# Two closing norms ordered anew, and returned rows gathered into the ring: a two-layer diffusion trunk with routed experts on one core

## The chip, the cores and the metric

The kernel runs on one core of a Trainium2 chip. It is one launch that computes the whole model below. The metric is the device time of a run in microseconds (us). A core has five engines that run their own instruction streams and wait for each other by semaphores: TensorE (PE in the profile: matrix products and transposes, results in PSUM), VectorE (DVE), ScalarE (ACT), GpSimd (POOL) and SyncE (SP, which here only issues transfers). Transfers (DMA) are issued from a queue of an engine (SPq, ACTq, POOLq) and run beside the engines.

## The reference, cut to what matters

There are 512 latent tokens and 256 context tokens of 1024 features, 32-bit floats, two layers. Layer 0 mixes tokens by windowed attention, layer 1 by a gated MLP over chunks of 128 tokens (gMLP); each is followed by a mixture of 16 experts in which each token goes to two.

```python
for i in range(DEPTH):                      # DEPTH = 2
    ...                                     # the mixer, its residual and norm
    y = routed_moe(tokens, router_w, router_bias, moe_w1[i], moe_w3[i], moe_w2[i])
    x = layer_norm(ALPHA * x + g_f * y[-B * L:].reshape(B, L, D), ln2_g[i], ln2_b[i])

def routed_moe(...):
    ...
    def expert_block(args):
        xb, e = args
        return (jax.nn.silu(xb @ w1[e]) * (xb @ w3[e])) @ w2[e]
    ys = lax.map(expert_block, (xs, blk_expert)).reshape(P, D)
    return jax.ops.segment_sum(ys * row_gate[:, None], row_tok, num_segments=T + 1)[:T]

def layer_norm(x, g, b):
    mu = mean(x); var = mean(square(x - mu))
    return (x - mu) * rsqrt(var + 1e-5) * g + b

def chunk_gmlp(h, w_in, b_in, ...):         # layer 1's mixer, h = x * (1 + scale) + shift
    z = gelu(h @ w_in + b_in)
    u, v = z[..., :1024], z[..., 1024:]
    ...
```

What matters here is the second norm of each layer ("closing norm"): it takes the sum of a token's residual and the two rows that its experts gave, and writes the normalised token. After layer 0 the gMLP's projection of `v` comes next; after layer 1 the result is the output.

## The kernel before, in words

**Tiles.** The 512 latent tokens are four tiles `X[0]` to `X[3]` of 128 tokens x 1024 features, held in SBUF (`x` in the rows). SBUF buffers come from pools: `slot` gives one of 28 buffers of 128 x 1024 ("the ring", for weights, split halves and much else), `uslot` one of 8 others. PSUM has three kinds of buffers, `pa` (128 x 1024), `pb` and `pt` (128 x 512), two of each.

**Experts.** `moe` (L1113 on) goes over a fixed list of units, each a number of rows for one expert: `gemm1`, `glu`, `gemm2` (`py`, a `pb` or `pa` buffer). The results of all units but the last two are multiplied by the gate (`ys`) and stored from POOL to a DRAM table `ydr` (L1070 to L1075). At unit n-2 `collect` (L1097) issues eight indirect DMAs on POOL: for each of the two experts of a token (`a` = 1, then `a` = 0) and each tile, the rows of the table that belong to its tokens come into a buffer `y`. They can start when the last store has landed. `combine` (L1106) is a DVE instruction per tile and `a`: X += y x gate; `a` = 1 stands before the last unit's `gemm2` in the program, `a` = 0 after it.

**The last two units** are not stored. Their result, times the gate (`ys`, L1154 for unit n-2 and L716 for n-1), is brought to the tokens by products with a one-hot matrix `oT` (`rows`, L681 to L685), two per tile for each of the two units, accumulated in PSUM; in the program and in PE's order those of unit n-2 (u = 0) come right behind that unit's work, those of unit n-1 (u = 1) behind `ys` of L716.

**The closing norm** (`last_norm`, L670). Per tile: two DVE additions of the PSUM halves to X with a running sum (`add`, L692), the mean (`mean`, L696), two squares with a sum on ACT (L699), the variance on DVE (`var`, L704 and L705). Then a reciprocal square root by Newton steps on DVE (`newton`, L730 to L742, some 14 tiny instructions), done for two tiles at a time (`norm`), and the normalisation on ACT: L1360 in layer 0, L1422 in layer 1.

**Behind the norm of layer 0** stands `pre(t)` for each tile: eight PE transposes (L1327) in two halves, a scale and shift out of PSUM on DVE (L1335, `ht`), a cast to the rounded type on ACT (L1339, `gh`), the remainder on DVE (L1340, `gl`), and two POOL instructions that apply the norm's own gain and bias to X (L1341, L1342). `vhalf(t, n)` is the projection of tile t to one half of `v`: 24 products (L428 to L430) over the eight blocks of features, three for each: `gh` x `wh`, `gh` x `wl`, `gl` x `wh`. The weights `winv` come in eight pieces; `split` (L221) casts a piece on ACT (`wh`, L224) and subtracts on DVE (`wl`, L225). Pieces 0 to 3 serve n = 0.

**Behind the norm of layer 1** the gain is multiplied on DVE (L1423) and the bias added (L1424): tiles 0 and 1 on POOL, tiles 2 and 3 on DVE. Then the output is stored from SP.

**What sets the order.** A scheduler of the tile framework orders each engine's stream by its own cost estimates; where `in_order` encloses code (all of `last_norm`, and `pre` and `vhalf` of n = 0), the named engines keep the program's order. SP issues weight pieces in a fixed list, as far as `limit` and the free buffers allow.

## Time and profile before

| | |
|---|---|
| median of 3 runs | 1209.11 us (1207.64 to 1211.41) |
| profiled execution | 1208.63 us, span from first to last instruction 1206.9 us |
| mean granted TensorE clock | 0.922 of full speed (2.4 GHz) |
| busy share of the span | PE 86%, PEld 49%, DVE 50%, ACT 29%, POOL 21% |
| DMA | 330.42 MB, mean 274 GB/s |
| closing norm of layer 0 | about 676 to 707 us, PE idle from 689.9 to 704.3 |
| closing norm of layer 1 | about 1166 us to the end, PE idle from 1173.6 |

The busy share is a mean over stages. The two closing norms are the two stretches late in a layer in which PE, elsewhere almost always busy, has nothing to do, so what ends there is read from the timeline of each engine and not from the shares. In a timeline row the first two numbers are the start and the busy time in us, counted from the span's start; `xN` is the number of instructions that the row joins; the bracket is the idle time before it and what ended it.

### The profile page before, as it was taken

Reading aid. Unit: us, or ns where it says so; the run is one execution under the profiler, and the core shown is the slowest. Engines: PE = TensorE matmul, PEld = TensorE weight load, DVE = VectorE, ACT = ScalarE, POOL = GpSimd, SP = SyncE. Lnnn points to the kernel's source line nnn. Section 1 sums busy time; section 2 is a strip of 40 time slices with the busy share of each in tenths; the row PEclk is TensorE's granted clock in tenths of the full one; section 3 lists DMA queues with packets and bytes.
Section 4 is the critical chain, followed back from the end, with each engine's and each line's share of the span. In section 5 each row is a group of like instructions: output and inputs, shape, how many; then the busy total and the mean of one; then the engine's idle time right before and its main releaser. Section 6 shows DMA issues by size and latency. Waiting matters only on the chain. (4 is left out here: it accounts for less than half of the span.)

```text
span 1206.9 us, 17614 instructions
## 1 busy us (share of the span) xinstructions
PE 1043.0 (86%) x6216; PEld 596.6 (49%) x6216; DVE 607.2 (50%) x1540; ACT 353.2 (29%) x716; POOL 253.0 (21%) x241
## 2 busy tenths in 40 slices
PE   6789778898898697999999769999859899999980
PEld 2567655554576233444344247888723344433430
DVE  1798899768346731211212597655565121221137
ACT  1553366776433111111101153532211011111103
POOL 0044424425000112331110343000011222211131
PEclk9898869999899798999999869999969899999995
DMA  8945776474467797999999803236489994899981
GB/s 337 402 152 179 263 271 189 139 259 166 137 217 283 253 384 259 390 410 410 410 410 410 293 1 140 88 101 208 177 307 412 347 410 160 351 410 409 410 329 70
DMA packets 103525, 330.42 MB, mean 274 GB/s; under 512 B 13040, under 2 KB 23744, under 8 KB 103424
## 3 DMA queue, kind: packets, MB, share of 16 engines
q1 hardware_dynamic: 88336, 287.43, 62.6%
q0 software_dynamic: 10512, 27.28, 6.1%
q10 hardware_dynamic: 4576, 14.45, 3.3%
q8 instruction: 53, 0.87, 0.3%
q14 instruction: 48, 0.39, 0.1%
HBM read 310.19 MB, written 22.06 MB: 275 GB/s over the span
## 5 line engine op out<-in xcount | busy, mean ns | idle before, releaser
L1031 PE MATMUL pb<-ring,xt 128*32 128x256 f32 (+1 forms) x1824 | 225.6, 467 | 11.5 <-DVEq L1253 10.8
L1031 PEld LDWEIGHTS pb<-ring,xt 128*32 128x32 f32 (+1 forms) x1824 | 83.3, 121 | 130.6 <-issue 83.9
L1042 DVE TENSOR_TENSOR si<-si,pb 128x256 f32<-128x256 f32 (+1 forms) x43 | 15.7, 365 | 223.2 <-ACT si L1041 223.2
L1075 POOL DMA_DIRECT2D ydr<-ys x114 | 58.1, 516 | 315.1 <-DVE ys L1070 229.9
L1064 PE MATMUL pb<-ring,hh 128*32 128x256 f32 (+1 forms) x912 | 113.2, 462 | 0.5 <-ACT hh L1053 0.5
L360 POOL TENSOR_TENSOR raw<-raw,row 128x1024 f32<-128x1024 f32 x28 | 78.2, 2801 | 108.7 <-DMA raw<-in_mt 81.1
L358 DVE SCALAR_TENSOR_TENSOR raw<-raw,row 128x1024 f32<-128x1024 f32 x52 | 91.0, 1764 | 0.0
L1041 ACT ACTIVATE si<-pb 128x256 f32<-128x256 f32 (+1 forms) x43 | 14.6, 339 | 232.5 <-PE pb L1031 232.5
L1031 PE MATMUL pa<-ring,xt 128*128 128x512 f32 x160 | 72.4, 600 | 0.0
L1064 PEld LDWEIGHTS pb<-ring,hh 128*32 128x32 f32 (+1 forms) x912 | 39.6, 119 | 58.3 <-issue 43.4
L994 POOL DMA_INDIRECT xg<-hdr,Rgi x22 | 23.2, 1056 | 213.6 <-DVE peb L868 124.6
L225 DVE TENSOR_TENSOR wl<-raw,wh 128x1024 fp32r<-128x1024 f32 x44 | 56.7, 1318 | 9.2 <-ACT wh L224 9.1
L558 DVE TENSOR_SCALAR_CACHE_REDUCE P<-pa,nsink 128x512 f32<-128x512 f32 (+1 forms) x64 | 50.9, 811 | 20.2 <-PE pa L554 8.1
L1053 ACT COPY hh<-pt 128x256 f32<-128x256 f32 (+2 forms) x48 | 17.0, 354 | 147.5 <-PE pt L1051 147.5
L1013 DVE TENSOR_SCALAR xt<-pt,gc,bc 128x128 f32<-128x128 f32 x88 | 30.1, 404 | 51.5 <-PE pt L1005 51.5
L560 ACT ACTIVATE P<-P,nm 128x512 f32<-128x512 f32 (+1 forms) x64 | 49.5, 775 | 14.3 <-DVE P L558 14.1
L1070 DVE TENSOR_TENSOR ys<-pb,gfs 128x512 f32<-128x512 f32 (+1 forms) x39 | 22.1, 567 | 58.4 <-PE pb L1064 58.4
L1011 ACT ACTIVATE xt<-pt,bc,gc 128x128 f32<-128x128 f32 x88 | 33.1, 456 | 59.5 <-PE pt L1005 38.9
L1031 PEld LDWEIGHTS pa<-ring,xt 128*128 128x128 f32 x160 | 29.1, 190 | 40.1 <-issue 39.9
L593 PE MATMUL pt<-cc,P 128*128 128x128 f32 x288 | 45.4, 290 | 4.0 <-ACT PT L594 3.6
L593 PEld LDWEIGHTS pt<-cc,P 128*128 128x128 f32 x288 | 32.4, 146 | 31.6 <-issue 26.0
L594 ACT COPY PT<-pt 128x512 f32<-128x512 f32 x72 | 39.4, 580 | 28.7 <-PE pt L593 28.7
(366 smaller groups left out, 2046.1 us busy)
## 6 DMA issues: line engine op xcount, KB each, us to landing
ring<-in_moe SPq DMA_DIRECT2D x336, 512.0 KB, 10.6
raw<-in_mt SPq DMA_DIRECT2D x80, 512.0 KB, 5.3
raw<-in_moe SPq DMA_DIRECT2D x48, 512.0 KB, 6.5
raw<-in_mod SPq DMA_DIRECT2D x16, 512.0 KB, 10.2
raw<-in_qkv SPq DMA_DIRECT2D x12, 512.0 KB, 10.2
ydr<-ys POOLq DMA_DIRECT2D x42, 128.0 KB, 5.4
ydr<-zero SPq DMA_DIRECT2D x10, 512.0 KB, 8.0
raw<-in_wo SPq DMA_DIRECT2D x8, 512.0 KB, 5.3
```

The lines of the kernel that those rows point to most:

```text
L225: V.tensor_sub(lo, src, hi.bitcast(F32))
L358: V.scalar_tensor_tensor(w, w, 1.0, srow[0], op0=OP.mult, op1=OP.mult, accum_out=mv[l][:, j:j + 1])
L360: GP.tensor_mul(w, w, srow[0])
L558: V.tensor_scalar(P[j], reg, -0.125, nsink[:, p * 8 + j:p * 8 + j + 1], op0=OP.mult, op1=OP.min, accum_out=nm[:, j:j + 1])
L560: SC.activation(P[j], P[j], AF.Exp, bias=nm[:, j:j + 1], scale=-1.0, accum_out=sums[:, j:j + 1])
L593: PE.transpose(pt[:, j * 128:(j + 1) * 128], P[a * 4 + j][:, i * 128:(i + 1) * 128], idf)
L594: cp = SC.copy(tl[:, a, :], pt)
L1011: SC.activation(o, i, AF.Identity, bias=b, scale=g)
L1013: V.tensor_scalar(o, i, g, b, op0=OP.mult, op1=OP.add)
L1031: PE.matmul(o.rearrange("p (m c) -> p m c", m=2), xt[:, k, c:c + n], w[:, h], start=(k == 0), stop=(k == 7), skip_group_check=True)
L1064: PE.matmul(o, ht[f], w[:, h], start=(f == 0), stop=(f == 3), skip_group_check=True)
L1075: GP.dma_start(ydr[row:row + n, h * n * 8:(h + 1) * n * 8], ys[h * n:h * n + n, :])
```

## The change

There are four parts.

1. **Layer 0, weights.** Pieces 0 to 3 of `winv` are loaded and split ahead of the gathers in the program. The SP loads of pieces 4 to 7 wait until the last gather (`got`) has landed.
2. **Buffers.** In layer 1 the gathered rows of `a` = 1 go to the ring (`slot`), not to `uslot`.
3. **Order inside the closing norm.** `combine` and both `ys` are moved into `last_norm`, in one fixed DVE order: four combines (`a` = 1), `ys` of unit n-2, two combines (`a` = 0), `ys` of unit n-1, two combines. The one-hot products of unit n-2 come behind its `ys`, so behind the first four combines.
4. **What follows the sums** is a function of the layer. `middle` (layer 0): sums of tiles 0 to 2, the norm of tiles 0 and 1, sums of tile 3, the norm of tiles 2 and 3. `end` (layer 1): sums of all tiles, one Newton chain for four tiles; z = (X - mean) x gain before the chain's result is known, then z x rstd + bias, both DVE; tile 1's last step is done on PE as bias (through the identity) plus a diagonal matrix of rstd times z, and copied out by ACT. The POOL additions and ACT normalisations of layer 1 are gone.

```diff
@@ issue (SP's weight list)
             wdma[0] = SP.dma_start(t, src)
+            if p[0] == "winv" and p[1] > 3:
+                after(wdma[0], RT[0]["got"], mybir.DependencyClass.Sync)
@@ moe
-        limit[0] = len(pieces) if l else pos["winu", 0]
+        limit[0] = len(pieces) if l else pos["winv", 4]
...
             elif i == n - 2:
-                R["yp"] = slot([128, 512], F32, "ys")
-                V.scalar_tensor_tensor(R["yp"], py, R["gs"][:, 0:1], gf[64], op0=OP.mult, op1=OP.mult)
+                R["py"] = py
...
             if i == n - 2:
-                collect(l, 1, uslot)
+                for p in [("winv", j) for j in range(4) if not l]:
+                    issue(pos[p] + 1)
+                    pairs[p] = split(raws[p])
+                collect(l, 1, slot if l else uslot)
                 collect(l, 0, slot)
-            if i == n - 1:
-                combine(l, 1, X)
+                limit[0] = max(limit[0], pos["winu", 0])
...
-        combine(l, 0, X)
@@ last_norm
         with in_order(PE, V, SC):
-            V.scalar_tensor_tensor(ys, py, R["gs"][:, 1:2], gf, op0=OP.mult, op1=OP.mult)
-            for t in range(4):
-                rows(t, 1, ys)
-            for t in range(4):
-                add(t, 0)
-                add(t, 1)
-                mean(t)
-            r = norm(0), norm(1)
-        return r
+            combine(l, 1, X, 0, 4)
+            for u, p in enumerate((R["py"], py)):
+                V.scalar_tensor_tensor(ys[u], p, R["gs"][:, u:u + 1], gf, op0=OP.mult, op1=OP.mult)
+                for t in range(4):
+                    rows(t, u, ys[u])
+                if u == 0:
+                    combine(l, 0, X, 0, 2)
+            combine(l, 0, X, 2, 4)
+            finish(X, sums, norm, nmu)
@@ layer 0
+    def middle(X, sums, norm, nmu):
+        def pair(t):
+            y = norm(t, t + 2)
+            nmr = small([128, 2], F32, "xm")
+            V.tensor_mul(nmr, nmu[:, t:t + 2], y)
+            for i in range(2):
+                SC.activation(X[t + i], X[t + i], AF.Identity, bias=nmr[:, i:i + 1], scale=y[:, i:i + 1])
+        for t in range(3):
+            sums(t)
+        pair(0)
+        sums(3)
+        pair(2)
@@ layer 1
-            SC.activation(x, x, AF.Identity, bias=nmr[:, i:i + 1], scale=y[:, i:i + 1])
-            V.tensor_mul(x, x, g2)
-            (GP if t == 0 else V).tensor_add(x, x, b2)
-            SP.dma_start(out[0, (t + i) * 128:(t + i + 1) * 128, :], x)
+    def end(X, sums, norm, nmu):
...
+        def scaled(t):
+            V.scalar_tensor_tensor(z[t], X[t], nmu[:, t:t + 1], g2, op0=OP.add, op1=OP.mult)
+        def done(t, y):
+            V.scalar_tensor_tensor(z[t], z[t], y[:, t:t + 1], b2, op0=OP.mult, op1=OP.add)
+            SP.dma_start(out[0, t * 128:(t + 1) * 128, :], z[t])
+        for t in range(4):
+            sums(t)
+        p = psA()
+        for ns in halves:
+            PE.matmul(p[:, ns], idf, b2[:, ns], start=True, stop=False, skip_group_check=True)
+        scaled(0)
+        scaled(1)
+        y = norm(0, 4)
+        V.tensor_scalar(dg, idf, y[:, 1:2], None, op0=OP.mult)
+        for ns in halves:
+            PE.matmul(p[:, ns], dg, z[1][:, ns], start=False, stop=True, skip_group_check=True)
+        done(0, y)
+        for ns in halves:
+            SC.copy(o[:, ns], p[:, ns])
+        SP.dma_start(out[0, 128:256, :], o)
+        for t in (2, 3):
+            scaled(t)
+            done(t, y)
```

How the instructions stand now, at three places. First DVE in the closing norm of layer 0, before (x_2832 to x_2835 are the four token tiles, L225 the subtraction of a weight piece, L1110 a combine, L1154 and L716 the two `ys`):

```order
L1154 SCALAR_TENSOR_TENSOR ys_6525<-pb_6516,gs_6253,gfs_3404 128x512
L225 TENSOR_TENSOR wl_6556<-raw_6420,wh_6555 128x1024
L225 TENSOR_TENSOR wl_6560<-raw_6424,wh_6559 128x1024
L1110 SCALAR_TENSOR_TENSOR x_2832<-y_6459,pg_5494,x_2832 128x1024
L225 TENSOR_TENSOR wl_6564<-raw_6428,wh_6563 128x1024
L225 TENSOR_TENSOR wl_6568<-raw_6432,wh_6567 128x1024
L716 SCALAR_TENSOR_TENSOR ys_6599<-pb_6536,gs_6253,gfs_3404 128x512
L1110 SCALAR_TENSOR_TENSOR x_2833<-y_6463,pg_5494,x_2833 128x1024
L1110 SCALAR_TENSOR_TENSOR x_2834<-y_6467,pg_5494,x_2834 128x1024
L1110 SCALAR_TENSOR_TENSOR x_2835<-y_6471,pg_5494,x_2835 128x1024
L1110 SCALAR_TENSOR_TENSOR x_2832<-y_6475,pg_5494,x_2832 128x1024
L1110 SCALAR_TENSOR_TENSOR x_2833<-y_6479,pg_5494,x_2833 128x1024
```

and after the change (the same are L227, L1112 and L720):

```order
L227 TENSOR_TENSOR wl_6452<-raw_6420,wh_6451 128x1024
L227 TENSOR_TENSOR wl_6456<-raw_6424,wh_6455 128x1024
L227 TENSOR_TENSOR wl_6460<-raw_6428,wh_6459 128x1024
L227 TENSOR_TENSOR wl_6464<-raw_6432,wh_6463 128x1024
L1112 SCALAR_TENSOR_TENSOR x_2832<-y_6467,pg_5494,x_2832 128x1024
L1112 SCALAR_TENSOR_TENSOR x_2833<-y_6471,pg_5494,x_2833 128x1024
L1112 SCALAR_TENSOR_TENSOR x_2834<-y_6475,pg_5494,x_2834 128x1024
L1112 SCALAR_TENSOR_TENSOR x_2835<-y_6479,pg_5494,x_2835 128x1024
L720 SCALAR_TENSOR_TENSOR ys_6588<-pb_6532,gs_6253,gfs_3404 128x512
L1112 SCALAR_TENSOR_TENSOR x_2832<-y_6483,pg_5494,x_2832 128x1024
L1112 SCALAR_TENSOR_TENSOR x_2833<-y_6487,pg_5494,x_2833 128x1024
L720 SCALAR_TENSOR_TENSOR ys_6589<-pb_6546,gs_6253,gfs_3404 128x512
```

The four subtractions stand together ahead of the combines; the `ys` of unit n-2 has moved from the front to behind four combines. The same order of combines and `ys` holds in layer 1, without the weights.

Second, PE in the projections that follow, before (L1327 is the transpose; pb_6753 is tile 0's half, pb_6810 tile 1's):

```order
L429 MATMUL pb_6753<-wl_6568,gh_6582 128x512
L430 MATMUL pb_6753<-wh_6567,gl_6583 128x512
L1327 MATMUL pt_6780<-cc,x_2834 128x128 x4
L428 MATMUL pb_6810<-wh_6555,gh_6576 128x512
L429 MATMUL pb_6810<-wl_6556,gh_6576 128x512
L430 MATMUL pb_6810<-wh_6555,gl_6577 128x512
L428 MATMUL pb_6810<-wh_6555,gh_6576 128x512
```

and after (L1329 the transpose; pb_6809 is tile 1's half, pb_6866 tile 2's):

```order
L431 MATMUL pb_6809<-wl_6464,gh_6572 128x512
L432 MATMUL pb_6809<-wh_6463,gl_6573 128x512
L1329 MATMUL pt_6779<-cc,x_2834 128x128 x4
L1329 MATMUL pt_6793<-cc,x_2834 128x128 x4
L430 MATMUL pb_6866<-wh_6451,gh_6566 128x512
L431 MATMUL pb_6866<-wl_6452,gh_6566 128x512
L1329 MATMUL pt_6836<-cc,x_2835 128x128 x4
```

Before, tile 2's first transposes stand ahead of tile 1's products and its second ones fourteen rows further, among them. Now both stand behind the last product of tile 1, and the next products are those of tile 2 itself. ACT's normalisation of tiles 2 and 3 has moved as well, behind the first gelu.

Third, DVE at the end of layer 1, before (L741, L742 and L712 end the second Newton chain; L1423 is the gain, L1424 the bias):

```order
L741 SCALAR_TENSOR_TENSOR xny_11278<-xnu_11283,xny_11278 128x2
L742 TENSOR_SCALAR xny_11278<-xny_11278 128x2
L712 TENSOR_TENSOR xm_11294<-xn_11196,xny_11278 128x2
L1423 TENSOR_TENSOR x_2834<-x_2834,row_11191 128x1024
L1423 TENSOR_TENSOR x_2835<-x_2835,row_11191 128x1024
L1424 TENSOR_TENSOR x_2834<-x_2834,row_11193 128x1024
L1424 TENSOR_TENSOR x_2835<-x_2835,row_11193 128x1024
```

and after (L743 and L744 end the only chain, width 4; L1454 is the diagonal, L1438 `scaled`, L1441 `done`):

```order
L743 SCALAR_TENSOR_TENSOR xny_11269<-xnu_11274,xny_11269 128x4
L744 TENSOR_SCALAR xny_11269<-xny_11269 128x4
L1454 TENSOR_SCALAR dg_11227<-cc,xny_11269 128x128
L1441 SCALAR_TENSOR_TENSOR z_11222<-z_11222,xny_11269,row_11182 128x1024
L1438 SCALAR_TENSOR_TENSOR z_11224<-x_2834,xn_11185,row_11180 128x1024
L1441 SCALAR_TENSOR_TENSOR z_11224<-z_11224,xny_11269,row_11182 128x1024
L1438 SCALAR_TENSOR_TENSOR z_11225<-x_2835,xn_11185,row_11180 128x1024
L1441 SCALAR_TENSOR_TENSOR z_11225<-z_11225,xny_11269,row_11182 128x1024
```

Two full-width instructions per tile are left on DVE for tiles 2 and 3 behind the chain, one for tile 0 and none for tile 1.

## Rows read from the trace of the kernel before

**Rows 1.** The chain of waits at the end: start us, length us, what

```profile
1191.14 2.23 DVE xny L741
...
1193.39 2.27 DVE xnu L739
```

**Rows 2.** Timeline of POOL at the end of layer 1

```profile
1190.02 5.61 POOL L1424 TENSOR_TENSOR x<-x,row 128x1024 f32<-128x1024 f32 x2 [18.55 <-DVE xnu L740]
```

**Rows 3.** Timeline of DVE at the end of layer 1

```profile
1166.58 0.75 DVE L716 SCALAR_TENSOR_TENSOR ys<-pb,gs,gfs 128x512 f32<-128x512 f32 x1 [2.68 <-PE pb L1064]
...
1169.32 8.96 DVE L1110 SCALAR_TENSOR_TENSOR x<-y,pg,x 128x1024 f32<-128x1024 f32 x7 [0.28 <-DMA y<-ydr,prow]
...
1178.20 0.69 DVE L692 SCALAR_TENSOR_TENSOR x<-pa,x 128x512 f32<-128x512 f32 x1
...
1184.07 0.20 DVE L704 TENSOR_SCALAR xv<-xq 128x1 f32<-128x1 f32 x1
...
1184.80 0.17 DVE L730 TENSOR_SCALAR xny<-xv 128x2 int32<-128x2 int32 x1
...
1187.18 0.16 DVE L712 TENSOR_TENSOR xm<-xn,xny 128x2 f32<-128x2 f32 x1
...
1200.68 2.35 DVE L1424 TENSOR_TENSOR x<-x,row 128x1024 f32<-128x1024 f32 x2
```

**Rows 4.** Timeline of PE, L684: warm in layer 1, cold in layer 0

```profile
1166.46 1.99 PE L684 MATMUL pa<-ys,oT 64*128 64x512 f32 x8
...
682.43 1.22 PE L684 MATMUL pb<-ys,oT 64*128 64x512 f32 x1 [2.89 <-DVE ys L716]
...
688.47 1.45 PE L684 MATMUL pb<-ys,oT 64*128 64x512 f32 x3
```

**Rows 5.** Windows: length, engines' busy time, granted clock, DMA share, GB/s

```profile
682.00:683.00 1.00, 0.57 (x2) 0.51 (x4) 1.00 (x2) 0.00 (x0) 0.58 (x1) 0.50 1.01 414
...
1176.00:1178.00 2.00, 0.00 (x0) 0.00 (x0) 2.00 (x2) 0.00 (x0) 0.00 (x0) 0.62 0.04 16
```

**Rows 6.** Timeline of SPq, POOL and ACT ahead of layer 0's norm

```profile
648.45 10.52 SPq L208 DMA_DIRECT2D raw<-in_winv  x8
...
662.55 0.54 POOL L1072 DMA_DIRECT2D ydr<-ys  x1 [13.55 <-DVE ys L1070]
...
671.26 1.06 POOL L1102 DMA_INDIRECT y<-ydr,prow  x1 [8.17 <-DMA ydr<-ys]
...
672.99 1.04 ACT L224 CAST wh<-raw 128x1024 fp32r<-128x1024 f32 x1 [1.11 <-issue]
```

**Rows 7.** The page, section 6: issues, KB each, median us to landing

```profile
ydr<-ys POOLq DMA_DIRECT2D x42, 128.0 KB, 5.4
```

**Rows 8.** Timeline of DVE in layer 0's norm

```profile
674.07 2.42 DVE L225 TENSOR_TENSOR wl<-raw,wh 128x1024 fp32r<-128x1024 f32 x2 [0.79 <-ACT wh L224]
...
678.16 1.28 DVE L1110 SCALAR_TENSOR_TENSOR x<-y,pg,x 128x1024 f32<-128x1024 f32 x1 [1.66 <-DMA y<-ydr,prow]
...
692.72 0.68 DVE L692 SCALAR_TENSOR_TENSOR x<-pa,x 128x512 f32<-128x512 f32 x1
...
699.66 0.20 DVE L704 TENSOR_SCALAR xv<-xq 128x1 f32<-128x1 f32 x1
```

**Rows 9.** Timeline of PE, DVE and POOL behind layer 0's norm

```profile
704.32 1.97 PE L1327 MATMUL pt<-cc,x 128*128 128x128 f32 x8 [14.41 <-ACT x L1360]
...
711.74 1.35 DVE L1335 TENSOR_SCALAR ht<-pt,gc,bc 128x128 f32<-128x128 f32 x4
...
716.14 3.38 DVE L1340 TENSOR_TENSOR gl<-ht,gh 128x256 fp32r<-128x256 f32 x2 [0.87 <-ACT gh L1339]
...
716.32 0.60 PE L1327 MATMUL pt<-cc,x 128*128 128x128 f32 x4
...
716.79 2.45 POOL L1342 TENSOR_TENSOR x<-x,row 128x1024 f32<-128x1024 f32 x1
...
719.58 0.50 PE L430 MATMUL pb<-wh,gl 128*128 128x512 f32 x1 [0.81 <-DVE gl L1340]
```

More of the change, by code (lines that the diff above doesn't have):

```diff
@@ L235, in ensure_split @@
                     return
-            else:
+            elif p not in pairs:
                 issue(nsplit[0] + 1)
@@ L668, in in_order, with last_norm @@
                     before[e] = i
-    def last_norm(l, X, py, gf):
+    def last_norm(l, X, py, gf, finish):
         R = RT[l]
@@ L675, in last_norm @@
         q = small([128, 4, 2], F32, "xq", 1)
-        v = [small([128, 3, 2], F32, "xv") for _ in range(2)]
+        v = small([128, 3, 4], F32, "xv", 1)
         o = [psA(), psA(), psT(), psT()]
         o = [[o[0][:, :512], o[0][:, 512:]], [o[1][:, :512], o[1][:, 512:]], o[2:], [psB(), psB()]]
-        ys = slot([128, 512], F32, "ys")
+        ys = [slot([128, 512], F32, "ys") for _ in range(2)]
         def rows(t, u, y):
@@ L685, in rows @@
                           start=(u == 0), stop=(u == 1))
-        for t in range(4):
-            rows(t, 0, R["yp"])
         def add(t, n):
@@ L702, in var, with norm, sums @@
         def var(t):
-            w = v[t // 2][:, 0, t % 2:t % 2 + 1]
+            w = v[:, 0, t:t + 1]
             V.tensor_scalar(w, q[:, t, 0:1], q[:, t, 1:2], 1.0 / D, op0=OP.add, op1=OP.mult)
             V.tensor_scalar(w, w, EPS, None, op0=OP.add)
-        def norm(i):
-            var(2 * i)
-            var(2 * i + 1)
-            y = newton([v[i][:, k] for k in range(3)], "x", 2)
-            nmr = small([128, 2], F32, "xm")
-            V.tensor_mul(nmr, nmu[:, 2 * i:2 * i + 2], y)
-            return y, nmr
-        with in_order(PE, V, SC):
-            V.scalar_tensor_tensor(ys, py, R["gs"][:, 1:2], gf, op0=OP.mult, op1=OP.mult)
-            for t in range(4):
-                rows(t, 1, ys)
-            for t in range(4):
-                add(t, 0)
-                add(t, 1)
-                mean(t)
-            r = norm(0), norm(1)
-        return r
+        def norm(a, b):
+            for t in range(a, b):
+                var(t)
+            return newton([v[:, k, a:b] for k in range(3)], "x", b - a)
+        def sums(t):
+            add(t, 0)
+            add(t, 1)
+            mean(t)
+        with in_order(PE, V, SC):
+            combine(l, 1, X, 0, 4)
[7 more added lines that the diff above has]
+            finish(X, sums, norm, nmu)
     def newton(v, w, n=1):
-        y = small([128, n], F32, w + "ny")
+        y = small([128, max(n, 4 * (n > 1))], F32, w + "ny")[:, :n]
         yi = y.bitcast(I32)
@@ L733, in newton @@
         V.tensor_scalar(v[2], v[0], 0.0625, None, op0=OP.mult)
-        u = small([128, n], F32, w + "nu")
+        u = small([128, max(n, 4 * (n > 1))], F32, w + "nu")[:, :n]
         for i in range(3):
@@ L1101, in collect, with combine @@
             R["y", t, a] = alloc([128, D], F32, "y")
-            GP.indirect_dma_start(out=R["y", t, a], out_offset=None, in_=ydr[:ZR[l] + 1, :],
-                                  in_offset=bass.IndirectOffsetOnAxis(ap=R["row"][:, a, t:t + 1], axis=0),
-                                  bounds_check=ZR[l], oob_is_err=False)
-    def combine(l, a, X):
+            R["got"] = GP.indirect_dma_start(out=R["y", t, a], out_offset=None, in_=ydr[:ZR[l] + 1, :],
+                                             in_offset=bass.IndirectOffsetOnAxis(ap=R["row"][:, a, t:t + 1], axis=0),
+                                             bounds_check=ZR[l], oob_is_err=False)
+    def combine(l, a, X, t0, t1):
         R = RT[l]
-        for t in range(4):
+        for t in range(t0, t1):
             V.scalar_tensor_tensor(X[t], R["y", t, a], R["g"][:, a, t:t + 1], X[t], op0=OP.mult, op1=OP.add)
@@ L1356, in vnorm @@
         SC.activation(v, v, AF.Identity, bias=nmr, scale=rstd)
-    for t, (y, nmr) in zip((0, 2), last_norm(0, X, py, gf)):
-        for i in range(2):
-            SC.activation(X[t + i], X[t + i], AF.Identity, bias=nmr[:, i:i + 1], scale=y[:, i:i + 1])
+    def middle(X, sums, norm, nmu):
[10 more added lines that the diff above has]
+        pair(2)
+    last_norm(0, X, py, gf, middle)
     with in_order(V, SC):
```

8 lines of the change are left out of this document (5 added, 3 removed).

## The prediction, made before the changed kernel was run

> **What bounds the kernel now.** I read the chain of waits first, then the timeline of each engine over the two closing norms, then windows for the clock and the transfers.
>
> The end of layer 1 is a DVE chain. In the chain of waits two instructions of two elements per partition hold 2.23 and 2.27 us [rows 1], where their like, the instruction that ends a Newton chain, takes 0.16 [rows 3]. In the same stretch POOL runs its two additions, 5.61 us from 1190.02 [rows 2], and the two DVE instructions end with POOL's. So DVE is held by POOL's work. The whole stretch from the first sum at 1178.20 to the last addition at 1200.68 + 2.35 = 1203.03 is 24.83 us [rows 3]; what follows (the last store) is 1206.9 - 1203.03 = 3.9 and stays.
>
> PE has no work in these stretches, and its clock shows it. At 682 to 683 it is granted 0.50, the lower of the two levels (1.2 GHz), after a wait of 2.89 us; at 1176 to 1178, with PE out of work, the mean is 0.62 [rows 4, 5]. At the full level four pairs of one-hot products take 1.99 us. At the lower one the stretch from 682.43 to 688.47 + 1.45 = 689.92 holds nine pairs in 7.49 us, the last of them fast again: some 0.84 a pair [rows 4].
>
> Layer 0's norm begins with transfers. The last store to the table is issued at 662.55, and the first gather begins 8.7 us later, released by its landing [rows 6], where the median store takes 5.4 [rows 7]: eight weight pieces were issued on SP from 648.45 on [rows 6]. The first combine still waits 1.66 us for its rows, and the sums start at 692.72 [rows 8]. PE, with nothing to do for 14.41 us, starts the transposes at 704.32 when ACT has normalised [rows 9]; from there PE is the bound, almost without gaps.
>
> **The change in layer 1: what it removes.** Counted behind the first sum. Four tiles of sums are unchanged: 1184.07 - 1178.20 = 5.87 us. Two `scaled` now stand next; seven combines, an instruction of the same shape and two SBUF inputs, take 8.96, so 1.28 each and some 1.2 without a wait: 2.4. They hide ACT's squares of the last tile. The variance costs 0.73 for two tiles (1184.07 to 1184.80), so 1.4 for four. One chain: 1187.18 - 1184.80 = 2.38; a width of four instead of two is not priced higher, since 0.16 for 128x2 is all overhead (bounds 0 and 0.5). The diagonal: 0.3. Then five full instructions, 6.1. Sum 5.9 + 2.4 + 1.4 + 2.4 + 0.3 + 6.1 = 18.5, so 6.3 us less than 24.83 [rows 3]. Of this 4.2 is the lock by POOL (2.23 + 2.27 - 2 x 0.16), the rest the second chain and the shorter tail. Tile 1's products and copies lie beside the five DVE instructions; without that cover they would cost some 3 us.
>
> **What it adds there.** The order of DVE is now four combines, `ys`, two combines, `ys`, two combines. Before, unit n-2's products ran right behind PE's last projection at 1166.46, at full clock [rows 4], beside the combines. Now they wait for `ys` behind the fourth combine: the second starts at 1169.32, so the fourth ends about 1173.2 and `ys` (0.75) at 1173.9 [rows 3]. PE has then been idle for over 7 us, longer than the 2.89 after which it was granted 0.50 [rows 4, 5]. So I take the low level: eight pairs at 0.84 make 6.7, the first tile's pairs of unit n-1 another 0.8, and the first sum starts at about 1181.5 instead of 1178.20: +3.3. Behind the waiting products stand only the next ones, and DVE's sums wait for them. The bounds: with PE not in the way DVE alone adds one `ys` twice, +1.5; with every pair slow to the last tile +5. Layer 1 together: -6.3 + 3.3 = -3.0 (from -4.8 to -1.3).
>
> **Layer 0, the front.** Weight pieces 4 to 7 are 2.1 MB, at the 414 GB/s of the window [rows 5] 5.1 us of transfers, and they leave the way of the store and the gathers. The store can win at most 8.7 - 5.4 = 3.3; I take 2.5 (bounds 0 and 3.3). The casts start about 1 us earlier, since the row loads that kept ACT before 672.99 [rows 6] now stand behind them, and the four subtractions, 2.42 a pair [rows 8], are done by 677.8. Then 4.9 for four combines and 0.75 for `ys`: 683.5. PE is cold as it was at 682.43: 6.7 for the block, 0.8 for tile 0: sums from 691.2. Before, they started at 692.72, with one more combine (1.2) still to come between, so 693.9 is what compares: -2.7. The norm of the first pair after three tiles instead of four saves one tile of sums, 5.87 / 4 = 1.5. The transposes start 4.2 earlier. SP's new wait has only pieces 4 to 7 behind it; they are used some 30 us later, and cost nothing.
>
> **Layer 0, the middle.** Tile 3's sums now delay ACT's normalisation of tile 2, and the scheduler has answered: both transposes of tile 2 stand behind the last product of tile 1, and tile 2's own products right behind them. Before, the first of them ran at 716.32 under tile 1's products, and the chain from a transpose to a product was hidden: the scale, 1.35 for four, a cast, a subtraction [rows 9]. Now PE waits for it, some 1.3 beyond what tile 3's transposes fill. And a subtraction was held when POOL's bias ran: a pair took 3.38 beside POOL's 2.45, some 2.4 more than free, and PE lost only 0.81 of it since it had other products [rows 9]. POOL's two instructions for tile 2 start as soon as its last transpose is done, now exactly when PE waits for these subtractions. I count one lock: 1.3 + 2.4 = 3.7. Bounds: 0 (all of it beside other work) and 6.1 (two locks). Layer 0 together: -4.2 + 3.7 = -0.5. Its bounds: with the store quickest (3.3 instead of 2.5) and no loss in the middle -5.0; with no gain by the store, so only the order's 1.5, and the middle as taken +2.2.
>
> The page SBUF — State Buffer of the Trainium skill, section Who interferes with whom, says that a DVE instruction with two SBUF inputs contends with a GpSimd instruction that reads SBUF, and that the one that comes second is fully blocked. The held DVE instructions of [rows 1, 9] agree. It speaks for the end of layer 1, where POOL's additions go, and against the middle of layer 0; by it alone each of tile 2's POOL instructions could hold a subtraction.
>
> **Sum.** -3.0 - 0.5 = -3.5 us against the profiled execution's 1208.63 (1206.9 span and 1.7 around it). The median of the runs is 0.5 above that execution, so 1209.11 - 3.5 = 1205.6. The rest of the trace keeps its order and is costed at nothing; ring buffers for layer 1's gathers are free at that point, since all weights have been loaded.
>
> **Rivals.**
> - *PE's one-hot products are not in the way* (the clock holds or they overlap better). For: at the full level eight pairs fit in 3.5 us, less than the four combines and two `ys` behind which they stand. Against: 0.50 after a shorter idle [rows 4, 5]. Layer 1 then wins 4.8, layer 0 another 1.7 more, 2.2: together -7.0, 1202.1.
> - *Layer 0's gathers come no sooner.* For: the store may wait for its own queue and not for the weights, and eight gathers are 4.2 MB by themselves. Against: 8.7 beside 5.4. Then the front wins only the 1.5 of the order, and layer 0 is +2.2, in all -0.8: 1208.3.
> - *Slower: POOL holds the subtractions of tiles 2 and 3 again and again.* Four POOL instructions meet eight subtractions there; three locks more than the one I count cost 3 x 2.4 = 7.2, and -3.5 + 7.2 = +3.7: 1212.8. From the second one on the change has lost its gain. For: a pair of 3.38 with PE waiting behind it [rows 9]. Against: between two POOL instructions DVE gets in, and only the first product of a block waits at once.
> - That the change does not do what it says is excluded by the order of the instructions for all but the wait for the last gather, which is the second rival.
>
> **How the numbers follow.** The forecast 0.42, PE not in the way 0.20, gathers no sooner 0.18, locks 0.17, something else 0.03. A measurement can tell about 0.3%, 3.6 us: faster is below 1205.5, slower above 1212.7. Of the forecast's own range, 1202.9 to 1208.3, half is faster. Faster: 0.21 + 0.20 = 0.41. Same: 0.21 + 0.18 + half of the locks 0.06 = 0.45. Slower: the other locks 0.11 and 0.03 = 0.14. The range from 1200.5 to 1211.0 leaves out the locks' upper part and the last of the first rival.
>
> **What would show it.** Right: no POOL addition and no tiny DVE instruction above 0.3 us behind layer 1's sums; 18 to 19 us from the first sum to the last DVE instruction; a granted clock of 0.50 in unit n-2's products of both layers, and a first sum there at 1181 on the old time base. In layer 0 a first gather some 2.5 us sooner behind the store, transposes about 4 sooner, and then a gap of PE of some 3 us behind tile 2's transposes. It is wrong if PE runs those products at the full level, if the middle shows no gap or several, or if layer 1's tail does not shrink by 6.

## The result, and the profile after

The changed kernel takes 1214.19 us (median of 7 runs, 1211.9 to 1214.97) against 1207.64 for the kernel before (7 runs); the ratio is 1.0056, with a 95% interval of 1.0035 to 1.0077. It is slower, by some 6.5 us. 1205.6 had been predicted, with a range up to 1211.0 and 0.14 for slower.

The profiled execution has a span of 1210.0 us, 3.1 more than before. The first 674 us were 1.9 shorter in this execution; the difference is there from 473 us on, long before the first transfer that the change moves (646 us). So I compare two stretches that begin with the end of PE's last expert product in a layer (`gemm2`; 675.91 and 674.05 in layer 0, 1166.54 and 1171.90 in layer 1), in us:

| stretch | before | after | predicted |
|---|---|---|---|
| layer 0: to the first transpose | 28.4 | 29.6 | 24.2 |
| layer 0: from there to the first product of the second half of `v` ("the middle") | 31.7 | 38.8 | 35.4 |
| layer 1: to the first sum | 11.7 | 14.9 | 15.0 |
| layer 1: first sum to last DVE instruction | 24.8 | 18.6 | 18.5 |
| layer 1: from there to the end | 3.9 | 4.6 | 3.9 |
| sum of the five | 100.5 | 106.5 | 97.0 |

Layer 1 came out as worked out, layer 0 did not.

**The end of layer 1.** DVE's timeline after the change, the rows that answer to [rows 3] (start, busy time, then as there):

```profile
1178.63 0.74 DVE L720 SCALAR_TENSOR_TENSOR ys<-pb,gs,gfs 128x512 f32<-128x512 f32 x1
...
1186.78 0.69 DVE L692 SCALAR_TENSOR_TENSOR x<-pa,x 128x512 f32<-128x512 f32 x1 [1.97 <-PE pa L687]
...
1198.88 0.29 DVE L1454 TENSOR_SCALAR dg<-cc,xny 128x128 f32<-128x128 f32 x1
...
1204.11 1.28 DVE L1441 SCALAR_TENSOR_TENSOR z<-z,xny,row 128x1024 f32<-128x1024 f32 x1
```

From 1186.78 to 1204.11 + 1.28 there is no tiny instruction of over 0.3 us left; [rows 1, 2] have no counterpart. The first sum waits 1.97 us for PE (its row above). PE's products of unit n-2 start only behind the fourth combine, after 7.53 us of idle time, at the lower clock level:

```profile
1179.43 3.79 PE L687 MATMUL pa<-ys,oT 64*128 64x512 f32 x8 [7.53 <-DVE ys L720]
...
1185.71 1.88 PE L687 MATMUL pa<-ys,oT 64*128 64x512 f32 x8
```

The window over them, with the columns of [rows 5], shows a granted clock of 0.50:

```profile
1180.00:1182.00 2.00, 2.00 (x6) 0.68 (x4) 2.00 (x3) 0.00 (x0) 0.00 (x0) 0.50 0.58 231
```

The sixteen records of unit n-2 take 6.28 us (1179.43 to 1185.71), where [rows 4] show eight of them in 1.99 at the full level. The prediction put 3.3 on this step; it measured 3.2. Of these, 1.97 is the wait for PE; the other 1.2 is DVE's own, whose last combine ends 12.9 us behind PE's last expert product instead of 11.7.

**Layer 0's front.** DVE, PE and ACT up to the first square:

```profile
675.55 2.47 DVE L1112 SCALAR_TENSOR_TENSOR x<-y,pg,x 128x1024 f32<-128x1024 f32 x2
678.87 1.28 DVE L1112 SCALAR_TENSOR_TENSOR x<-y,pg,x 128x1024 f32<-128x1024 f32 x1 [0.84 <-DMA y<-ydr,prow]
682.30 1.28 DVE L1112 SCALAR_TENSOR_TENSOR x<-y,pg,x 128x1024 f32<-128x1024 f32 x1 [2.15 <-DMA y<-ydr,prow]
...
684.30 3.79 PE L687 MATMUL pa<-ys,oT 64*128 64x512 f32 x8 [10.24 <-DVE ys L720]
...
687.98 8.28 ACTq L1122 DMA_DIRECT2D gfs<-mdr  x6
...
693.09 0.21 DVE L696 TENSOR_SCALAR xn<-xs 128x1 f32<-128x1 f32 x1
...
696.30 0.72 ACT L699 ACTIVATE sq<-x,xn 128x512 f32<-128x512 f32 x1 [22.50 <-DVE xn L696]
```

Two things were not foreseen. The third and fourth combine wait 0.84 and 2.15 us for gathered rows, and PE's products stand behind the fourth, so the first sum comes 0.3 us sooner than the like of [rows 8] and not 2.7 (17.7 behind PE's last expert product, against 16.8 with a combine of 1.2 still to come). And the first square starts 3.0 us behind the first mean, which is there at 693.09 + 0.21: ACT stands in six issues of transfers from 687.98 to 696.26. They load the next layer's gate row (`gfs`, L1122), whose buffer the last `ys` reads.

**Layer 0's middle.** PE's waits there, in a view that sums them (us in total, times, longest), before and after (9.4 of the first line after are the wait ahead of the first transpose, so outside the middle):

```profile
PE pb L430 <- DVE gl L1340: 1.3, 2, 0.8
```

```profile
PE pt L1329 <- ACT x L1366: 9.9, 2, 9.4
PE pb L432 <- DVE gl L1342: 3.9, 6, 0.9
PE pb L430 <- ACT gh L1341: 0.8, 1, 0.8
...
PE pt L1329 <- DVE ht L1337: 0.7, 1, 0.7
```

These waits explain only a part of the 7.1 us. PE's idle time in the middle rose from 1.7 to 6.4 us, its busy time from 30.0 to 32.4 for the same products: free products start 0.23 us apart with records of 0.39, so one that is held for less than 0.16 shows no wait, and every longer hold shows a shorter one.

Around tile 2's transposes PE waits for ACT's normalisation and then for the first cast:

```profile
723.93 1.09 PE L1329 MATMUL pt<-cc,x 128*128 128x128 f32 x8 [0.52 <-ACT x L1366]
725.84 0.50 PE L430 MATMUL pb<-wh,gh 128*128 128x512 f32 x1 [0.82 <-ACT gh L1341]
```

And the subtractions of tiles 2 and 3 on DVE, with POOL's instructions for tile 2 (they answer to the pair in [rows 9]):

```profile
725.17 2.36 POOL L1343 TENSOR_TENSOR x<-x,row 128x1024 f32<-128x1024 f32 x1 [6.51 <-PE pt L1329]
...
725.90 4.42 DVE L1342 TENSOR_TENSOR gl<-ht,gh 128x256 fp32r<-128x256 f32 x2
...
727.61 2.43 POOL L1344 TENSOR_TENSOR x<-x,row 128x1024 f32<-128x1024 f32 x1
...
734.90 3.08 DVE L1342 TENSOR_TENSOR gl<-ht,gh 128x256 fp32r<-128x256 f32 x2
```

Tile 2's pair takes 4.42 us, where a free one takes 0.98; it ends 0.3 us behind POOL's second instruction. Tile 3's pair takes 3.08 and ends the same 0.3 us behind POOL's second instruction for that tile (735.25 + 2.44).

### The profile page after: what moved, and what is told of

Read it like the earlier page. It is cut to its first block, busy times and chain, and to the rows that moved or that the text cites. A ratio compares the mean times of both kernels' runs of the same rounds, so it can differ in the third digit from the quotient of the medians.

```text
span 1210.0 us, 17625 instructions
## 1 busy us (share of the span) xinstructions
PE 1048.1 (87%) x6224; PEld 598.3 (49%) x6224; DVE 607.6 (50%) x1526; ACT 349.0 (29%) x714; POOL 251.6 (21%) x239
## 5 line engine op out<-in xcount | busy, mean ns | idle before, releaser
L362 POOL TENSOR_TENSOR raw<-raw,row 128x1024 f32<-128x1024 f32 x28 | 81.4, 2916 | 105.1 <-ACT kh L474 56.4
L227 DVE TENSOR_TENSOR wl<-raw,wh 128x1024 fp32r<-128x1024 f32 x44 | 54.3, 1268 | 12.0 <-ACT wh L226 12.0
L560 DVE TENSOR_SCALAR_CACHE_REDUCE P<-pa,nsink 128x512 f32<-128x512 f32 (+1 forms) x64 | 50.9, 810 | 18.5 <-PE pa L556 8.1
L1015 DVE TENSOR_SCALAR xt<-pt,gc,bc 128x128 f32<-128x128 f32 x88 | 30.1, 404 | 51.4 <-PE pt L1007 51.4
L1013 ACT ACTIVATE xt<-pt,bc,gc 128x128 f32<-128x128 f32 x88 | 33.1, 456 | 59.5 <-PE pt L1007 38.9
L1033 PEld LDWEIGHTS pa<-ring,xt 128*128 128x128 f32 x160 | 29.1, 190 | 40.1 <-issue 40.1
L605 PE MATMUL pb<-PT,Vt 128*64 128x512 f32 x144 | 39.7, 630 | 8.3 <-ACT PT L596 8.3
```

The lines of the kernel that those rows point to most:

```text
L227: V.tensor_sub(lo, src, hi.bitcast(F32))
L362: GP.tensor_mul(w, w, srow[0])
L560: V.tensor_scalar(P[j], reg, -0.125, nsink[:, p * 8 + j:p * 8 + j + 1], op0=OP.mult, op1=OP.min, accum_out=nm[:, j:j + 1])
L605: m.append(PE.matmul(po[a * 64:(a + 1) * 64, :], Vt[kb // 3][:, kb % 3, g * 64:(g + 1) * 64], tl[:, a, :], start=(i == 0), stop=(i == nb - ...
L1013: SC.activation(o, i, AF.Identity, bias=b, scale=g)
L1015: V.tensor_scalar(o, i, g, b, op0=OP.mult, op1=OP.add)
```

## The experiments

Each kernel was compared with the kernel before in alternating runs (in these the median of the kernel before was 1207.12 to 1208.18). "Front" is the first row of the table above, "middle" the second; layer 1 is the sum of its three rows; they are read from one trace of each kernel. Kernels whose front has the order of the changed kernel (pool_late, pool_late2, gain_on_dve) read 29.1 to 31.6 there, so a difference of a microsecond between two fronts says little.

| kernel | median us | ratio to before, 95% | front | middle | layer 1 |
|---|---|---|---|---|---|
| before | 1207.64 | | 28.4 | 31.7 | 40.4 |
| after | 1214.19 | 1.0056 (1.0035 to 1.0077) | 29.6 | 38.8 | 38.1 |
| layer1_only | 1205.02 | 0.9977 (0.9959 to 0.9995) | 28.2 | 31.8 | 36.9 |
| four_sums | 1208.12 | 1.0012 (0.9994 to 1.0030) | 29.8 | 33.3 | 37.1 |
| gfs_sp | 1210.66 | 1.0037 (1.0015 to 1.0059) | 27.3 | 39.3 | 37.3 |
| pool_late | 1213.29 | 1.0047 (1.0022 to 1.0071) | 31.6 | 38.9 | 38.3 |
| pool_late2 | 1210.1 (one run) | | 30.0 | 30.1 | 38.3 |
| no_got | 1211.87 | 1.0032 (1.0020 to 1.0043) | 27.5 | 39.1 | 38.6 |
| ys_first | 1210.67 | 1.0020 (1.0005 to 1.0035) | 29.4 | 38.8 | 34.9 |
| ys_first_four_sums | 1206.62 | 0.9978 (0.9963 to 0.9993) | 30.1 | 33.3 | 35.3 |
| no_got_ys_first | 1208.76 | 1.0013 (0.9996 to 1.0031) | 27.4 | 40.7 | 35.4 |
| no_locks_pool | 1205.86 | 0.9990 (0.9972 to 1.0008) | 27.4 | 31.0 | 35.2 |
| no_locks_dve | 1199.86 | 0.9945 (0.9923 to 0.9967) | 27.5 | 29.7 | 35.3 |
| gain_on_dve | 1202.48 | 0.9955 (0.9939 to 0.9972) | 29.1 | 30.6 | 37.2 |

**layer1_only: layer 0 as before.** Part 1, and parts 3 and 4 for layer 0, are taken back; parts 2, 3 and 4 stay for layer 1. Against the changed kernel, the main lines (the wait on `got`, the early `winv` splits and `middle`'s order go as well):

```diff
             elif i == n - 2:
                 R["py"] = py
+                if l == 0:
+                    R["yp"] = slot([128, 512], F32, "ys")
+                    V.scalar_tensor_tensor(R["yp"], py, R["gs"][:, 0:1], gf[64], op0=OP.mult, op1=OP.mult)
...
+        if l == 0:
+            for t in range(4):
+                rows(t, 0, R["yp"])
+            with in_order(PE, V, SC):
+                V.scalar_tensor_tensor(ys[0], py, R["gs"][:, 1:2], gf, op0=OP.mult, op1=OP.mult)
+                for t in range(4):
+                    rows(t, 1, ys[0])
+                finish(X, sums, norm, nmu)
+            return
```

> Layer 0 as before, layer 1 as in the changed kernel. I measure two stretches in a trace: layer 0's from the end of its last gemm2 to the first product of the second half of v (60.1 us before, 68.4 after), layer 1's from the end of its last gemm2 to the end of the span (40.4 before, 38.1 after). My theory (layer 0 lost 8.3 us, layer 1 won 2.3): 60.1 and 38.1, about 2.3 us faster than before, 1205. Rival (the loss is not in layer 0's closing but in the buffers or the order of layer 1): layer 1's stretch is not shorter than 40.4, or the run is as slow as the changed kernel, 1214.

Measured as expected: 1205.02, layer 0's two rows as before, layer 1's stretch 36.9. The loss is in layer 0.

**four_sums: the old order of the norms in layer 0.**

```diff
-        for t in range(3):
-            sums(t)
-        pair(0)
-        sums(3)
-        pair(2)
+        for t in range(4):
+            sums(t)
+        for t in (0, 2):
+            y = norm(t, t + 2)
+            nmr = small([128, 2], F32, "xm")
+            V.tensor_mul(nmr, nmu[:, t:t + 2], y)
+            normed.append((t, y, nmr))
```

> The changed kernel, but layer 0 sums all four tiles before the two norms, and ACT's normalisation stands outside the fixed order, as before. My theory: from the first transpose to the first product of the second half takes 31.7 us as before instead of 38.8, because tile 2's transposes stand again under tile 1's products; the first transpose comes up to 1.5 later; in all 5 to 6 us faster than the changed kernel, about 1208.5. Rival (GpSimd's lock on DVE costs by itself, whatever the order of the transposes): the stretch stays above 36 us. Rival (the load is late, not the order): no change, 1214.

ACT's normalisation follows behind `last_norm`, from `normed`. 1208.12 is what my theory said to 0.4 us, in part by luck. The middle is 33.3, not 31.7: tile 2's pair of subtractions still takes 3.10 us. Against that the front is only 0.2 later and not 1.5, and layer 1 is 1.0 shorter than in the changed kernel.

**gfs_sp: the gate loads on SP's queue.**

```diff
-                SC.dma_start(gf[n][h * n:h * n + n, :], gfr...)
+                (SP if l else SC).dma_start(gf[n][h * n:h * n + n, :], gfr...)
```

> The changed kernel, but the six loads of the next layer's gate row (L1122, which wait until the last ys has read the buffer) are issued on SP's queue instead of ACT's. My theory: they hold ACT until 3.0 us after the first tile's mean is known; without them the first square starts within 0.1 us of the mean, and the transposes 2.9 us sooner: about 1211. Rival (ACT waits for something else, or DVE's sums and not the squares set the norm): the first square or the transposes are no sooner, 1214.

The first square follows the first mean at once, and the front is 2.3 shorter; 1210.66. ACT's rows:

```profile
693.67 0.72 ACT L699 ACTIVATE sq<-x,xn 128x512 f32<-128x512 f32 x1 [20.07 <-DVE xn L696]
```

The mean is there at 693.63 (its instruction starts at 693.42 and takes 0.21).

**pool_late and pool_late2: POOL's gain and bias behind the first half of `v`.** Each tile's two POOL instructions leave `pre(t)`:

```diff
-        GP.tensor_mul(x, x, lg2)
-        GP.tensor_add(x, x, lb2)
...
         vhalf(3, 0)
+    late = V.tensor_copy(small([128, 1], F32, "lt", 1), vv[3][:, 0:1])
+    for x in X:
+        after(GP.tensor_mul(x, x, lg2), late, mybir.DependencyClass.Sync)
+        GP.tensor_add(x, x, lb2)
```

> The changed kernel, but GpSimd's two instructions per tile that apply gain and bias to X come behind the first half of v (a one-element copy on DVE releases them). My theory: the waits of PE for DVE's subtractions, 3.9 us in six places, go, the waits for transposes (10.5 with that at the start) and casts stay: the stretch from the first transpose shrinks from 38.8 to about 35, the run to about 1210.5. Rival (locks explain all of the middle's loss): it shrinks to 31.7 or below, 1207. Rival (locks hide beside other waits): it stays at 38, 1214.

In pool_late the order was given without a semaphore, and POOL's first instruction ran at 708.30, as early in the stretch as before the edit: nothing was tested.

> The edit of pool_late in a form that holds: there GpSimd's instructions still ran where they had run before, since only their place in the order was given; now they wait by a semaphore for a one-element DVE copy behind tile 3's gelu. The middle is read, not the total, since the eight instructions now meet the next weight pieces' subtractions. My theory: the six waits for subtractions (3.9 us) go, those for transposes and casts stay, and the middle (first transpose to the first product of the second half) shrinks from 38.8 to about 35. Rival (locks explain all of its loss): to 31.7 or below. Rival (they hide beside other waits): it stays at 38 or more.

My theory lost here and the rival won: the middle falls to 30.1, below that of the kernel before, though the transposes of tile 2 still stand late. The waits of PE in it:

```profile
PE pb L430 <- DVE v L1350: 5.9, 1, 5.9
PE pb L430 <- ACT gh L1341: 0.8, 1, 0.8
PE pt L1329 <- DVE ht L1337: 0.7, 1, 0.7
```

No wait for a subtraction is left. The first line is new and lies behind the middle: POOL's eight instructions now run from 736.69 to 755.48 and hold the Newton chain of `v`'s norm, whose instructions have one element per partition. The addition that PE waits for (L1350) stands behind this chain in DVE's order:

```profile
736.69 9.52 POOL L1386 TENSOR_TENSOR x<-x,row 128x1024 f32<-128x1024 f32 x4 [58.45 <-issue]
...
741.52 2.34 DVE L743 SCALAR_TENSOR_TENSOR cny<-cnu,cny 128x1 f32<-128x1 f32 x1
743.89 2.33 DVE L739 SCALAR_TENSOR_TENSOR cnu<-cny,cnv 128x1 f32<-128x1 f32 x1
746.26 2.32 DVE L743 SCALAR_TENSOR_TENSOR cny<-cnu,cny 128x1 f32<-128x1 f32 x1
```

**no_got: no wait for the last gather.**

```diff
-            if p[0] == "winv" and p[1] > 3:
-                after(wdma[0], RT[0]["got"], mybir.DependencyClass.Sync)
```

> The changed kernel without the wait of weight pieces 4 to 7 for the last gather: they are loaded as early as before. My theory: the store and the gathers share the transfers with them again, so the first gather comes 2 us later; against that the gate loads (L1122) no longer run beside them and hold ACT for some 3 us instead of 8.3; together within 2 us of the changed kernel, 1212 to 1216. Rival (the wait is the loss): layer 0's stretch falls below 65, about 1210. Rival (the wait is what the front wins by): above 70, 1217.

The first sum comes 18.4 behind PE's last expert product instead of 17.7, but ACT's six issues take 3.26 us instead of 8.28 and hold nobody: the front is 27.5. So the wait cost 3.0 on ACT. That it gained the 0.7 at the gathers is not shown: kernels that keep it, with the same order, have their first sum 15.8 to 18.7 behind. Nor are pieces 4 to 7 loaded as early as before, as I had expected: `limit` still holds them, and SP issues them from 664.53 to 667.43, behind the store (660.23). The first gather begins 6.6 us behind the store, against 6.8 with the wait and 8.7 before, so it is not the wait that brought the gathers forward; of part 1, `limit` is left.

**ys_first: both `ys` and their products ahead of the combines.** The products stood so before the change, those of both units behind the last expert product (1166.46 in [rows 4]); the kernel's description above, which has those of unit n-2 right behind that unit's own work, is wrong there.

```diff
-            combine(l, 1, X, 0, 4)
             for u, p in enumerate((R["py"], py)):
                 V.scalar_tensor_tensor(ys[u], p, R["gs"][:, u:u + 1], gf, op0=OP.mult, op1=OP.mult)
                 for t in range(4):
                     rows(t, u, ys[u])
-                if u == 0:
-                    combine(l, 0, X, 0, 2)
-            combine(l, 0, X, 2, 4)
+            combine(l, 1, X, 0, 4)
+            combine(l, 0, X, 0, 4)
```

> The changed kernel, but both ys and their one-hot products stand ahead of the eight combines in both layers, as the order was before. My theory: the products run at full clock under the combines, the gate loads go out some 10 us sooner and hold nobody; layer 0's first sum comes 15 us after gemm2 instead of 17.7, the first transpose 24 instead of 29.6, the middle stays at 38.8; layer 1's first sum 11.7 instead of 14.9: 1206 in all. Rival (the gathered rows come too late for the order to matter): first sums within 0.7 us of the changed kernel's, 1213. Rival (only the gate loads matter): like gfs_sp, layer 1 unchanged, 1211.

Layer 1 is as expected: the products run at the full level right behind the expert's, the first sum comes 11.7 behind them, 3.2 sooner. In layer 0 the front stays, since ACT is held longer still, and the median is 1210.67 and not 1206:

```profile
1171.34 1.99 PE L687 MATMUL pa<-ys,oT 64*128 64x512 f32 x8
...
676.75 19.06 ACTq L1120 DMA_DIRECT2D gfs<-mdr  x6
```

The six issues start 2.9 us behind PE's last expert product, 11 sooner than in the changed kernel, and end 22.0 behind it (695.81), where they ended there too (22.2). So it is not their buffer that holds them. The order of the program with its waits names what it is: the fifth and sixth gate load wait for the semaphores that weight pieces 4 and 5 are issued under.

```
SP   L208  DMA raw_6507<-in_winv 128x1024 [waits DMAHW7_49,DMASW7_49,PE_49]
SP   L208  DMA raw_6509<-in_winv 128x1024 [waits DMAHW0_49,PE_49]
ACT  L1120 DMA gfs_8104<-mdr 32x256 [waits DMAHW7_49]
ACT  L1120 DMA gfs_8104<-mdr 32x256 [waits DMAHW0_49]
```

In these traces there are eight such semaphores for all queues of SP and ACT, and a transfer waits until the one before it under its own has landed: the pieces are issued at 690.05 and 690.47, the two gate loads at 693.58 and 695.51. Pieces 4 and 5 wait for the last gather (`DMASW7`), so the gate loads do too, and ACT with them. Before, pieces 4 and 5 were under the semaphores 2 and 3 and had landed long ago.

**ys_first_four_sums.** Both edits.

> ys_first and four_sums together: what is left of the change is the new end of layer 1, the ring buffers and the weight pieces ahead of the gathers. My theory: layer 0's stretch 58 to 59 us (60.1 before), layer 1's 35.3 (40.4 before): 1200 to 1202, faster than before and than layer1_only (1205). Rival (the two edits win the same time): not below 1206.

A miss: 1206.62, not 1200 to 1202. The front is 30.1, for the same hold of ACT, which I had thought gone with the earlier `ys`, and the middle 33.3 as in four_sums. The rival's number (not below 1206) came and its reason did not: the two gains add up, with a layer 1 that is 5.1 us shorter than before beside the shorter middle.

**no_got_ys_first.** Both edits, to test the semaphores.

> no_got and ys_first together. In ys_first the six gate loads went out at 676.8 and held ACT until 695.9, 19 us; my theory is now that their fifth and sixth wait for a transfer semaphore that they share with weight pieces 4 and 5, which wait for the last gather. Without that wait: the issues take 3.3 us and are over by 681, the first square comes with the first mean (1.6 us behind the first sum), the first transpose 9.1 behind the first sum (27 behind gemm2 instead of 29.4), the middle stays at 38.8, layer 1's stretch at 35: 1207 to 1208. Rival (the gate loads wait for bandwidth or for their buffer): ACT is held as long as in ys_first and the first transpose stays at 29.4: 1210.

The front is 27.4: the issues take 5.85 us and are over by 685.0, and the first square follows the first mean. The median is 0.8 above what was expected. The middle is 40.7 in this trace, 1.9 longer than in ys_first, and its trace shows why: ACT's normalisation of tiles 2 and 3 stands ahead of the first gelu here, not behind it, so DVE waits for the gelu ahead of tile 2's scale:

```profile
725.47 0.69 DVE L642 BATCH_NORM_STATS2 cst<-v 128x6 f32<-128x512 f32 x1 [3.42 <-ACT v L1349]
```

PE then waits 2.85 us for tile 2's first cast and 1.26 for a subtraction, and its granted clock is 0.50 again from 730 to 733 and 0.51 from 733 to 736, where ys_first's trace has 1.00.

**no_locks_pool and no_locks_dve: the locks taken out of the middle.** no_got_ys_first, with POOL's eight instructions behind tile 0's second half of `v`, or with the same arithmetic on DVE:

```diff
     for t in range(4):
-        vhalf(t, 1)
+        f = vhalf(t, 1)             # now returns its DVE addition
         vnorm(t)
+        after(V.tensor_mul(X[t], X[t], lg2), f)
+        V.tensor_add(X[t], X[t], lb2)
```

> no_got_ys_first, with GpSimd's eight instructions released only behind tile 0's second half of v, when the next weight pieces have been subtracted. My theory since pool_late2 (middle 30.1): the locks are all of the middle's loss, and there they met pieces 4 to 7 instead (7.7 us lost behind it); here they meet little that PE waits for: middle 30 to 31, layer 0's stretch 57 to 58, at most 2 us lost behind it: 1199 to 1201. Rival (wherever the eight instructions run, some DVE work on the path is held): 5 us or more lost behind the stretch, 1204 or later.

The rival won: the middle is 31.0, but the 430.5 us behind it become 438.7, since the Newton chain of `v`'s norm is held here as in pool_late2.

```profile
742.27 9.50 POOL L1386 TENSOR_TENSOR x<-x,row 128x1024 f32<-128x1024 f32 x4 [59.46 <-DMA raw<-in_winu]
...
744.73 2.33 DVE L739 SCALAR_TENSOR_TENSOR cny<-cnu,cny 128x1 f32<-128x1 f32 x1
747.10 2.34 DVE L735 SCALAR_TENSOR_TENSOR cnu<-cny,cnv 128x1 f32<-128x1 f32 x1
```

> no_got_ys_first, with the gain and the bias of layer 0's norm on DVE instead of GpSimd (eight instructions of 1.2 us, two behind each second half of v), so that nothing is left to lock. My theory: middle 30 to 31, layer 0's stretch 57 to 58, behind it at most 1 us more than the 430.5 of before, layer 1's stretch 35: 1199 to 1200, faster than both kernels. Rival (10 us more of DVE work hold the norm of v or the weights): 3 us or more lost behind the stretch, 1203 or later.

As expected but for 0.2 us behind the middle: 1199.86, 0.9945 of before (0.9923 to 0.9967), faster than both kernels. The middle is 29.7, and 1.2 us are given back behind it.

**gain_on_dve: the same edit alone on the changed kernel.**

> The changed kernel with one edit: the gain and the bias of layer 0's norm on DVE behind each second half of v, none on GpSimd. My theory now: the locks alone turned the change from faster to slower; the front keeps its loss (first transpose 29.6 behind gemm2), the middle falls from 38.8 to 29.7 to 30.5, at most 1.5 us are given back behind it, layer 1 stays at 38: some 8 us faster than the changed kernel, 1205 to 1207, at or below before. Rival (the new order of the transposes has a price of its own): the middle stays above 33, 1209 or later.

1202.48, 2.5 us below the range expected: 0.9955 of before (0.9939 to 0.9972), where the changed kernel stands at 1.0056. The middle is 8.2 us shorter than there, the five stretches 9.6 us. PE's waits in the middle:

```profile
PE pb L430 <- ACT gh L1341: 0.8, 1, 0.8
PE pt L1329 <- DVE ht L1337: 0.7, 1, 0.7
```

No wait for a subtraction is left, with the transposes in the new order. PE's idle time in the middle is 1.5 us instead of 6.4, its busy time 29.1 instead of 32.4.

## Why the prediction was wrong

- **Layer 1, right.** The tail was forecast at 18.5 and is 18.6, the first sum 3.3 later and is 3.2 later: 1.97 by waiting for PE at the lower clock level as argued, 1.2 by DVE's own order. ys_first, which takes back both, gives just these 3.2 back. The agreement to 0.1 has luck in it, since kernels with the same order read 13.3 to 15.3 for the first sum (last section). Missed: 0.7 at the end, where the stores of tiles 1, 2 and 3 are now issued within 2 us of each other; that this is the reason is not tested.
- **Layer 0's middle, a step that failed.** "I count one lock: 1.3 + 2.4 = 3.7." The mechanism was right and its count was not: the middle lost 7.1, and with POOL's instructions out of it the changed kernel's takes 30.1 (pool_late2) to 30.6 (gain_on_dve), so the locks cost 8.2 to 8.6 there, not 2.4. The third rival ("POOL holds the subtractions of tiles 2 and 3 again and again", four locks, 9.6) is nearer to that, and had 0.17. That its time of 1212.8 is near the measured 1214.19 is in part luck: it took layer 0's front as forecast, which came out 5.4 worse. I had argued against it that DVE gets in between two POOL instructions. It does, with one instruction, and the next is held again: tile 2's pair took 4.42. A subtraction that waits 2.4 holds PE only as far as PE has no other product; before, PE's waits for subtractions were only 1.3 us in all, and that cover went with the new place of tile 2's transposes (with the old place, in four_sums, the middle is 33.3 with POOL still at work). The other term, 1.3 for the transposes themselves, is there: 0.52 + 0.82. With POOL gone, 0.8 of it is left (gain_on_dve, whose middle is 1.1 shorter than before). Whether the new order of the transposes would still lose to the old one without POOL is not shown, since no run has the old order without POOL.
- **Layer 0's front, the other step that failed.** -4.2 was forecast and +1.2 measured. Of the 5.4, 3.0 is ACT's hold by the gate loads, which the prediction had at nothing (SP's new wait has "only pieces 4 to 7 behind it" and would "cost nothing"): a shared semaphore and not a queue put two gate loads behind that wait, and I had followed SP's queue only. Wherever the wait stands and ACT issues the loads, the first square comes 3.0 to 4.5 us behind the first mean; without the wait (no_got and the three kernels built on it) or with the loads on SP (gfs_sp) it comes within 0.1. The loads themselves were late because `ys` was, which the prediction moved without asking who waits for its buffer; but in ys_first they start 11 us sooner and end no sooner. gfs_sp and no_got each win 2.1 to 2.3 of it. The remaining 2.4 are combines that waited for rows, a wait that the prediction's "4.9 for four combines" left out. The first gather did come 1.9 us sooner behind the store (6.8 instead of 8.7), but the fourth combine, forecast to end 6.8 us behind PE's last expert product, ended 9.5 behind it, and `ys` and PE's products stand behind it. The wait that cost ACT the 3.0 was not needed for the sooner gather: without it the gather came 6.6 behind the store, with pieces 4 to 7 still held by `limit`. Of the 1.5 for three tiles of sums instead of four, 1.3 came: from the first sum to the first transpose it is 9.1 in gfs_sp, against 11.6 before, 1.2 of which was a combine.
- **The rule on the shared port.** The Trainium skill's page SBUF — State Buffer, section Who interferes with whom, says that a VectorE instruction with two SBUF inputs contends with a GpSimd instruction that reads SBUF. The prediction read from it that each of tile 2's POOL instructions could hold a subtraction, and counted one; the trace shows both (4.42 for the pair). The held instructions of one element per partition (2.33 us), which have two SBUF inputs, agree with the rule.

## What to carry to other kernels

Where GpSimd works on SBUF beside VectorE, check every two-input VectorE instruction on the path for a hold; here one lasted up to what was left of GpSimd's instruction (2.3 of 2.4 us). What decided the price was whether the engine behind had other work at that moment: a new order of that engine's work turned hidden holds into time (1.3 to 3.9 us of waits), and moving the GpSimd work elsewhere on GpSimd only moved them (7.8 and 8.2 us behind the middle). Eight full instructions more on VectorE were cheaper here than eight on GpSimd. When a transfer is made to wait, look up which other transfers share its semaphore, on any queue.

## What was not expected of the hardware

- A hold does not shrink with the instruction that is held: 2.33 us at 128 x 1 (0.16 to 0.22 free), and POOL's eight instructions of pool_late2 hold five of them in a row, one each.
- A one-input instruction was held too: in the changed kernel's middle a TENSOR_SCALAR on 128 x 2 integers took 2.33 us beside POOL's second instruction of tile 0 and ended with it. It is so in all six traces in which the two meet, and 0.16 in the four that have no POOL instruction there; its like on 128 x 1 ran in 0.14 beside POOL in pool_late2.

```profile
708.18 2.43 POOL L1344 TENSOR_TENSOR x<-x,row 128x1024 f32<-128x1024 f32 x1
...
708.30 2.33 DVE L732 TENSOR_SCALAR xny<-xv 128x2 int32<-128x2 int32 x1
```

- The first sum of layer 1 lies between 13.3 and 15.3 us behind PE's last expert product in the kernels that share its order, mostly by the clock and not by the gathers. In all of them the last combine ends 12.7 to 13.2 behind it; the first sum then waits for PE 0.64 to 0.84 us in the early ones and 1.67 to 2.10 in the late ones. From 10 to 12 us behind the last expert product the granted clock is 0.95 in layer1_only (first sum at 13.3) and 0.50 in the changed kernel (14.9). Why the full level comes back sooner in some traces stays open.
